# A gated-linear-attention trunk on one core: turning two blocks of rows into columns with 32x32 squares on VectorE

## The chip, the cores and the metric

The kernel runs on one core of a Trainium2 chip. The metric is device time in microseconds (us): the median of three runs. PE is TensorE, DVE is VectorE, ACT is ScalarE, POOL is GpSimd; SP is the engine whose queue issues every DMA of this kernel.

## The reference

One decoder layer on 2048 tokens of 1024 features: gated linear attention, then a gated FFN with a causal convolution, each modulated before (`1 + scale`, `shift`) and normalised after. What matters here is the seam between the two: the attention's normalised rows go through the FFN's modulation and then into a matmul.

```python
def post_norm_residual(x, cs, w_mod, b_mod, ln_gain, ln_bias, sublayer):
    shift, scale, gate = jnp.split((cs @ w_mod + b_mod)[:, None, :], 3, axis=-1)
    y = sublayer(x * (1 + scale) + shift)
    return layer_norm(DN_ALPHA * x + (1 + gate) * y, ln_gain, ln_bias)

def gla_mixer(h, w_in, w_a2, b_a, norm_g, w_o):          # shortened
    q, k, v, r, a_lr = jnp.split(h @ w_in, [qk, 2 * qk, 2 * qk + dv, 2 * qk + 2 * dv], axis=-1)
    log_a = jax.nn.log_sigmoid((a_lr @ w_a2 + b_a)) / GLA_TAU
    # 4 heads, chunks of 64 tokens: att = causal(q_dec k_inv^T); o = att v + q_dec S; S = S * decay + k_dec^T v
    o = o * lax.rsqrt(jnp.mean(o * o, -1, keepdims=True) + LN_EPS) * norm_g
    return (o * jax.nn.silu(r)) @ w_o

def conv_ffn(h, w_up, conv_w, conv_b, w_down):
    u, g = jnp.split(h @ w_up, 2, axis=-1)
    u = causal_depthwise_conv3(u, conv_w) + conv_b
    return (jax.nn.silu(u) * g) @ w_down

x = post_norm_residual(x, cs, mod_w[i, 0], mod_b[i, 0], ln_g[i, 0], ln_b[i, 0], mixer)
x = post_norm_residual(x, cs, mod_w[i, 1], mod_b[i, 1], ln_g[i, 1], ln_b[i, 1], ffn)
```

## The kernel before

**Arithmetic.** Each f32 operand is split into a high part (an ACT cast) and a remainder (a DVE subtraction, line 110), and a product is three matmuls (lines 113 to 115), 128x128 by 128x512.

**Attention.** The tokens go in four blocks of 512 (`tb` 0 to 3, here blocks 1 to 4). Each block runs through 32 weight units of 1 MB (`unit()`): for each pair of heads four of v, then q and k of each head and the r gate; after those eight of the output projection. A unit is loaded by SP into one of four buffers `hl` (line 136, from `wq_d` in block 4), so a load waits until the buffer's last reader on PE is done. Units 0 to 3 of block 4 are v of the first two heads, 4 and 5 q and k of head 0, 6 and 7 q and k of head 1. The work of head 0 beside them is `head_a` (four transposes at line 713, then the products Q by KI) and `head_b` (the products of v by KTt). `at_unit` hangs other work on units of the stream.

**Rows and columns.** The output projection leaves rows: 128 tokens by 1024 features, four tiles `z` for a block. `ln1` normalises them (BN statistics on DVE, the scaling on ACT, line 863) and stores them to `zn_d`. The FFN needs columns: features on the partitions, tokens along the row, times `1 + scale` plus `shift` (`A2`, `B2`). `ln1_out` makes these: a 128x128 transpose on PE with the identity (line 844) into a PSUM bank, four for a tile `kt` of 128 features, then one eviction that also scales and shifts (DVE line 849, or ACT line 847), and a store of 256 KB to `xm2_d` (line 850). Block 1 is turned from reloaded rows (`zc`, line 838), blocks 2 and 3 from the `z` tiles at two units in the next block (for block 3 that is after units 2 and 3 of block 4), block 4 from `zc` in FFN iterations 3 to 6, one pair of tiles in each.

**Token sums.** The FFN is a fast matrix product with seven products of half the size for eight, over two halves of the tokens. `x_pre` makes four of its operands for a half and a pair: four 512 KB loads `xp` from `xm2_d` (line 275), four DVE subtractions (line 281), each with a store to `xt_d` behind it (lines 283 to 289). For the first half it is hung on block 4 (units 4 and 13), for the second on FFN iterations 9 and 12 (`todo`).

**FFN up.** 44 iterations, 22 for each half of the tokens, of seven products of twelve matmuls. The list `todo` hangs the turning on them. In each iteration `w_load` brings the next up-weights (`wu`, `wg`, lines 333 and 334), whose sums are made on DVE an iteration later.

**Order.** The kernel is written as a program; a scheduler of the framework puts each engine's instructions into an order by its own costs, and then each engine runs its order strictly. SP too: a store that waits for DVE holds up every load behind it. `order(later, earlier)` fixes two instructions against each other without a wait.

Of the kernel before, what the change touches and what calls it, by code (L numbers as in the profile page):

```python
# [8 lines left out]
F32 = mybir.dt.float32  # L9
F32R = mybir.dt.float32r  # L10
U32 = mybir.dt.uint32
AF = mybir.ActivationFunctionType
# [4 lines left out]
P = 128  # L17
# [21 lines left out]
def kernel(  # L39
# [46 lines left out]
    def raw_tile(name="raw"):  # L86
        return rawp.tile([P, 1024], F32, tag="raw", name=name)

    def z_tile(name="z"):
        return zp.tile([P, 1024], F32, tag="z", name=name)  # L90
# [21 lines left out]
    def mm3(po, a, b, first, last, resumed=False):  # L112
        nc.tensor.matmul(po, a[0], b[0], start=first, stop=False, skip_group_check=resumed)  # L113
        nc.tensor.matmul(po, a[0], b[1], start=False, stop=False, skip_group_check=resumed)  # L114
        return nc.tensor.matmul(po, a[1], b[0], start=False, stop=last, skip_group_check=resumed)  # L115
# [81 lines left out]
    ws_d = [dram.tile([P, 2, 512], F32, name=f"ws_d{j}") for j in range(NJ)]  # L197
    xt_d = [[[dram.tile([P, 1024], F32, name=f"xt_d{h}_{i}_{r}") for r in range(2)] for i in range(7)] for h in range(2)]
    wq_d = [dram.tile([P, 2, 1024], F32, name=f"wq_d{n}") for n in range(32)]
    xm2_d = [[dram.tile([P, 2, TB], F32, name=f"xm2_d{t}_{k}") for k in range(4)] for t in range(NTB)]  # L200
    G2_d = dram.tile([P, D], F32, name="G2_d")

# [67 lines left out]

    X_AT = ((0, 0), (1, 0), (1, 1), (0, 1))

    def x_raw(hf, n, pr, r):
        half, b = X_AT[n]
        load(r, xm2_d[2 * hf + b][2 * half + pr].rearrange("p k t -> p (k t)"))

    def x_pre(hf, pr):
        b11, b21, b22, b12 = [z_tile("xp") for _ in range(4)]
        for n, r in ((0, b11), (3, b12), (2, b22), (1, b21)):
            x_raw(hf, n, pr, r)  # L280
        sub = lambda o, a, b: nc.vector.tensor_tensor(o, a, b, op=ALU.subtract)
        sub(b11, b12, b11)
        store(xt_d[hf][4][pr], b11)
        sub(b12, b22, b12)
        store(xt_d[hf][6][pr], b12)
        sub(b22, b22, b11)
        store(xt_d[hf][5][pr], b22)
        sub(b21, b21, b22)
        store(xt_d[hf][3][pr], b21)
# [73 lines left out]
    def at_unit(u, fn, *a):  # L363
        steps.setdefault(u, []).append((fn, a))
# [11 lines left out]
    if True:  # L376
# [288 lines left out]
        def gemm_f(xm):  # L665
            w = unit()
            wv = w.rearrange("p s (k c) -> p s k c", k=KT)
            po = psum("mm", 4)
            for kt in range(KT):
                mm3(po, (wv[:, 0, kt], wv[:, 1, kt]), (xm[kt][:, 0], xm[kt][:, 1]), kt == 0, kt == KT - 1)  # L670
            return po

        def gemm_q(xm, E, tick, pq=None):
# [159 lines left out]
        def ln1_out(tb, zs, prs, by_act=False):  # L833
            for pr in prs:
# [4 lines left out]
                for k in range(2):  # L839
# [9 lines left out]
                        nc.vector.tensor_scalar(xt, pt, A2[:, kt:kt + 1], B2[:, kt:kt + 1], op0=ALU.mult, op1=ALU.add)  # L849
                    store(xm2_d[tb][pr][:, k], xt)  # L850

        def normalise(z, after=None):
            st = smp.tile([P, 2, 6], F32, tag="bst", name="bst")
            for i in range(2):
                bn = nc.vector.bn_stats(st[:, i], z[:, i * 512:i * 512 + 512])
                if after is not None:
                    order(bn, after)
            mv = smp.tile([P, 2], F32, tag="mv", name="mv")
            nc.vector.bn_aggr(mv, st)
            rs = smp.tile([P, 2], F32, tag="rs", name="rs")  # L860
            rsqrt_eps(rs[:, 0:1], mv[:, 1:2])
            nc.gpsimd.tensor_scalar(rs[:, 1:2], mv[:, 0:1], rs[:, 0:1], -1.0, op0=ALU.mult, op1=ALU.mult)
            nc.scalar.activation(z, z, AF.Identity, bias=rs[:, 1:2], scale=rs[:, 0:1])
# [28 lines left out]
        for tb in range(NTB):  # L892
            last = tb + 1 == NTB
            b = 32 * tb
            gated = []
            Hs = [dict(h=h, last=last, gated=gated) for h in range(NH)]
            for i, u in ((0, 6), (1, 8), (2, 18), (3, 20)):
                u += b + (tb == 0 and i < 2)
                for k, f in ((0, head_a), (1, head_b), (3, head_c), (5, head_d)):
                    at_unit(u + k, f, Hs[i])  # L900
            at_unit(b + 12, next_decays, (2, 3))
            if tb == 0:
                for k, u in enumerate((10, 10, 11, 11, 11, 12, 14, 15)):
                    at_unit(u, gate_step, 0, k, gs1)
                at_unit(16, gate_end, 0, G1, gs1)
            if tb == 1:
                load(lnc, lncol)
                for n in range(16):
                    at_unit(b + 5 + n, mod_cols, 1, n // 4, (n % 4,))
                    if n % 4 == 3:  # L910
                        at_unit(b + 6 + n, mod_fin, 1, n // 4)
                at_unit(b + 22, mod2)
            if tb == 2:
                for pr in range(4):
                    at_unit(b + 13 + pr, ln1_out, 0, None, (pr,))
                for k in range(8):
                    at_unit(b + 14 + k, gate_step, 1, k, gs2)
                at_unit(b + 22, gate2)
            if tb == 3:
                at_unit(b + 4, x_pre, 0, 0)  # L920
                at_unit(b + 13, x_pre, 0, 1)
                at_unit(b + 25, first_w)
                at_unit(b + 29, lambda: (w_sums1(first["W"]), w_h0(first["W"])))
                at_unit(b + 30, lambda: (w_sums2(first["W"]), w_h2(first["W"])))
            if not last:
                if tb == 0:
                    for pr in range(4):
                        at_unit(b + 25 + pr, next_xm, tb + 1, (pr,))
                else:
                    at_unit(b + 25, next_xm, tb + 1)  # L930
                at_unit(b + 28 + (tb == 0), next_a)
                at_unit(b + 29 + (tb == 0), next_decays, (0, 1))

            pqk = {}
            if tb == 0:
                xm, nxt["A3"], v0, pqk["pq"], pqk["pk"] = gemm_start()
                next_decays((0, 1))
            else:
                v0 = gemm_v(xm, tick)
            for pr in range(2):  # L940
                v = v0 if pr == 0 else gemm_v(xm, tick)
                E = nxt["E"]
                for h in (2 * pr, 2 * pr + 1):
                    H = Hs[h]
                    H["v"], H["el"] = v, E[h][2]
                    H["Q"] = gemm_q(xm, E[h], tick, pqk.pop("pq", None))
                    H["KI"], H["KK"] = gemm_k(xm, E[h], tick, pqk.pop("pk", None))
                for h in (2 * pr, 2 * pr + 1):
                    Hs[h]["sr"] = []
                    for e in range(2):  # L950
                        Hs[h]["sr"].append(gemm_r(xm, tick))
            zs = load_z(tb)
            if 0 < tb < NTB - 1:
                at_unit(b + 32 + 2, ln1_out, tb, zs, range(0, 2))
                at_unit(b + 32 + 3, ln1_out, tb, zs, range(2, 4))
            out_proj(tb, 0, gated, zs, tick)
            if last:
                abx.close()
                up = ctx.enter_context(tc.tile_pool(name="up", bufs=1, reuse_waits="tile"))
                X0, XN = [None] * 7, [None] * 7  # L960
                for i in PROD[:4]:
                    tiles = [x_tile(up, i) for pr in range(2)]
                    x_fill(up, X0, i, x_stage(up, 0, i), tiles)
            out_proj(tb, 1, gated, zs, tick)
            if last:
                zs_last = zs
            else:
                xm = nxt["xm"]
# [11 lines left out]
    if True:  # L980
# [15 lines left out]
        def prod(st, i, po, first):  # L996
            h, half = WHERE[i]
            t = st["W"][h]
            w = [(t[:, 0, half * 512 + k * P:half * 512 + k * P + P],
                  t[:, 1, half * 512 + k * P:half * 512 + k * P + P]) for k in range(4)]  # L1000
            mm = mmk(po, w, st["X"][i], first)
            if st["refill"] is not None:
                x_fill(up if i in PROD[:4] else ur, st["refill"], i, ahead_x.pop(0))
                if len(nextx) > 0:
                    ahead_x.append(x_stage(up, 1, nextx.pop(0)))
            return mm
# [110 lines left out]
        w_h3(W)  # L1117

        nextx, ahead_x = list(PROD), []
        todo = {3 + pr: [(ln1_out, NTB - 1, None, (pr,), True)] for pr in range(4)}  # L1120
        todo |= {9: [(x_pre, 1, 0)], 12: [(x_pre, 1, 1)]}
        G2 = gp.tile([P, D], F32, tag="G", name="G2")
        load(G2, G2_d)
        prev = None
        for n in range(2 * NJ):
# [41 lines left out]
            if prev is not None:  # L1167
                conv_b(prev["h1"], prev["U"], 1, prev["j"])
            pc = st["pc"] = psum("w", 4)
            prod(st, 4, pc, True)  # L1170
            prod(st, 6, pa, False)
            u3, u3i = keep(pa, "u3")
            if prev is not None:
# [245 lines left out]
```

## Time and profile before

| What | Value |
|---|---|
| Median of 3 runs | 2142.45 us (2142.05 to 2142.62) |
| The profiled execution's own time | 2141.68 us |
| Its span | 2139.8 us |
| Granted TensorE clock | 0.998 of full speed |
| Busy: PE, DVE, ACT, POOL | 99%, 67%, 42%, 5% |
| DMA queue of SP | 69.9% of 16 engines |
| Chain that ended last | PE 92%, DVE 3%, DMA 3% |

The trace's times count from the span's start. A matmul of 128x512 shows 0.39 us but follows the last one after 0.227 us, as they overlap; what a group of PE instructions costs is therefore read from the starts of those around it. The span, 2139.8 us, is 1.9 us under the execution's time.

### The profile page before, as it was taken

The page shows a single profiled execution, that of the slowest core. Times are in us where ns is not written, and L with a number is a line of the kernel's source. Part 1 is how long each engine was busy: PE and PEld are TensorE (multiplying, and loading weights), DVE is VectorE, ACT ScalarE, POOL GpSimd, SP SyncE. Part 2 cuts the span into 40 slices and gives each one's busy share as a digit, 9 for nine tenths or more (in the row PEclk, how much of TensorE's full clock was granted, in tenths as well). Part 3 has the DMA queues.
Part 4 walks back from the last instruction along what each step waited for, and adds up shares of the span by engine and source line. Part 5 has one row for each costly group of instructions (what it writes and reads, how often), then busy time and mean ns, then how long its engine had stood idle before and what let it go on. Part 6 is the DMA issues. An engine that isn't in the chain of part 4 may idle for free.

```text
span 2139.8 us, 26750 instructions
## 1 busy us (share of the span) xinstructions
PE 2124.7 (99%) x9916; PEld 1771.1 (83%) x9916; DVE 1423.3 (67%) x2015; ACT 892.6 (42%) x1356; POOL 115.5 (5%) x258
## 2 busy tenths in 40 slices
PE   9999999999999999999999999999999999999998
PEld 7888888888888888888888888888888888888886
DVE  7876576434743553878777778666666797578557
ACT  4655553433343343544444454333333434344332
POOL 0010100010001000000000000000000000021003
PEclk9999999999999999999999999999999999999999
DMA  8477886664866766777855469878777888577562
GB/s 313 165 259 271 315 325 238 222 249 176 296 228 240 263 243 230 256 260 279 308 191 186 172 214 340 295 247 284 249 263 278 268 309 287 193 243 254 191 204 89
DMA packets 155106, 529.28 MB, mean 247 GB/s; under 512 B 17664, under 2 KB 21888, under 8 KB 134752
## 3 DMA queue, kind: packets, MB, share of 16 engines
q1 hardware_dynamic: 154976, 527.58, 69.9%
q8 instruction: 78, 1.28, 0.2%
q14 instruction: 52, 0.43, 0.1%
HBM read 364.72 MB, written 162.79 MB: 247 GB/s over the span
## 4 chain that ended last, share of the span: by engine, by line
PE 92%; DVE 3%; DMA 3%; ACT 1%; issue 1%; SPq 0%; POOL 0%; POOLq 0%; DVEq 0%; ACTq 0%
PE ps_mm L113 22%; PE ps_mm L115 22%; PE ps_mm L114 22%; PE ps_w L114 8%; PE ps_w L115 8%; PE ps_w L113 8%; DMA raw<-in_wab_dram 2%; DMA xraw<-in_xT_dram 1%; PE ps_w L844 1%; DVE hl L110 1%; PE ps_w L602 1%; PE ps_w L793 1%; ACT hl L107 0%; PE ps_w L529 0%; PE ps_w L528 0%
## 5 line engine op out<-in xcount | busy, mean ns | idle before, releaser
L113 PE MATMUL ps_mm<-xc,hl 128*128 128x512 f32 x704 | 274.3, 390 | 0.0
L114 PE MATMUL ps_mm<-xc,hl 128*128 128x512 f32 x704 | 273.9, 389 | 0.0
L115 PE MATMUL ps_mm<-xc,hl 128*128 128x512 f32 x704 | 273.9, 389 | 0.0
L113 PE MATMUL ps_mm<-xm,hl 128*128 128x512 f32 x496 | 194.9, 393 | 0.5 <-DVE v L110 0.5
L115 PE MATMUL ps_mm<-xm,hl 128*128 128x512 f32 x496 | 193.6, 390 | 0.0
L114 PE MATMUL ps_mm<-xm,hl 128*128 128x512 f32 x496 | 193.5, 390 | 0.0
L113 PEld LDWEIGHTS ps_mm<-xc,hl 128*128 128x128 f32 x704 | 132.1, 188 | 27.5 <-ACT u L1010 0.2
L115 PEld LDWEIGHTS ps_mm<-xc,hl 128*128 128x128 f32 x704 | 132.1, 188 | 27.5
L114 PEld LDWEIGHTS ps_mm<-xc,hl 128*128 128x128 f32 x704 | 132.2, 188 | 27.3
L1024 DVE SCALAR_TENSOR_TENSOR ct<-U,cw_sb,ct 128x512 f32<-128x512 f32 x176 | 131.6, 747 | 22.1 <-ACT ct L1018 20.6
L113 PE MATMUL ps_w<-xc,hl 128*128 128x512 f32 x352 | 136.9, 389 | 0.0
L114 PE MATMUL ps_w<-xc,hl 128*128 128x512 f32 x352 | 136.9, 389 | 0.0
L115 PE MATMUL ps_w<-xc,hl 128*128 128x512 f32 x352 | 136.9, 389 | 0.0
L107 ACT CAST dhl<-raw 128x1024 fp32r<-128x1024 f32 x57 | 60.0, 1053 | 152.3 <-PE ps_mm L115 96.0
L1010 ACT COPY u<-ps_mm 128x512 f32<-128x512 f32 x88 | 51.4, 584 | 154.9 <-PE ps_mm L115 152.9
L107 ACT CAST hl<-raw 128x1024 fp32r<-128x1024 f32 (+1 forms) x73 | 70.0, 965 | 108.8 <-PE ps_mm L115 42.2
L110 DVE TENSOR_TENSOR hl<-raw,hl 128x1024 fp32r<-128x1024 f32 (+1 forms) x73 | 81.0, 1116 | 47.3 <-ACT hl L107 47.1
L110 DVE TENSOR_TENSOR dhl<-raw,dhl 128x1024 fp32r<-128x1024 f32 x57 | 69.5, 1219 | 63.8 <-ACT dhl L107 63.8
L115 PEld LDWEIGHTS ps_mm<-xm,hl 128*128 128x128 f32 x496 | 93.2, 188 | 19.9 <-issue 0.2
L113 PEld LDWEIGHTS ps_mm<-xm,hl 128*128 128x128 f32 x496 | 93.2, 188 | 19.7 <-DVE v L110 1.0
L114 PEld LDWEIGHTS ps_mm<-xm,hl 128*128 128x128 f32 x496 | 93.2, 188 | 18.2 <-issue 0.2
L113 PE MATMUL ps_mm<-dhl 128*128 128x512 f32 x264 | 102.7, 389 | 0.0
(246 smaller groups left out, 4998.0 us busy)
## 6 DMA issues: line engine op xcount, KB each, us to landing
hl<-wq_d SPq DMA_DIRECT2D x82, 1024.0 KB, 5.0
hc_d<-ct SPq DMA_DIRECT2D x154, 256.0 KB, 2.6
raw<-hc_d SPq DMA_DIRECT2D x70, 512.0 KB, 4.2
draw<-wc_d SPq DMA_DIRECT2D x70, 512.0 KB, 4.8
wq_d<-hl SPq DMA_DIRECT2D x32, 1024.0 KB, 5.1
raw<-in_wab_dram SPq DMA_DIRECT2D x46, 512.0 KB, 6.4
wu<-in_wup_dram SPq DMA_DIRECT2D x44, 512.0 KB, 5.6
wg<-in_wup_dram SPq DMA_DIRECT2D x44, 512.0 KB, 4.0
```

Source lines behind the costliest of these rows:

```text
L107: accs["copy"] = nc.scalar.copy(h, src)
L110: return nc.vector.tensor_tensor(l, src if lsrc is None else lsrc, h.bitcast(F32), op=ALU.subtract)
L113: nc.tensor.matmul(po, a[0], b[0], start=first, stop=False, skip_group_check=resumed)
L114: nc.tensor.matmul(po, a[0], b[1], start=False, stop=False, skip_group_check=resumed)
L115: return nc.tensor.matmul(po, a[1], b[0], start=False, stop=last, skip_group_check=resumed)
L602: nc.tensor.matmul(po, wv[:, a, kt], xm[kt][:, b], start=kt + a + b == 0, stop=kt == KT - 1 and b == 1)
L793: nc.tensor.transpose(pt[:, s * P:s * P + P], on[:, s, e * P:e * P + P], ident)
L844: nc.tensor.transpose(pt[:, t * P:t * P + P], src, ident)
L1010: return t, nc.scalar.copy(t, po)
L1024: nc.vector.scalar_tensor_tensor(ct, U[:, o + i:o + i + 512], cw_sb[:, j, i:i + 1], ct, op0=ALU.mult, op1=ALU.add)
```

## The change

Blocks 3 and 4 are no longer transposed on PE. DVE transposes each 32x32 square of a row tile and leaves it where it stands (`nc.vector.transpose`, an instruction STREAM_TRANSPOSE of 128x1024): of block 3 into a raw tile `zt` after units 1 and 2 of block 4, of block 4 onto its own `z` tile in FFN iterations 2 to 5. The result goes to a new DRAM tensor `zt_d` in four stores of 512 KB for a block. A column tile `kt` is read back by four DMAs (`cols_in`), each for 32 features by 512 tokens, which put every square in its place: 512 pieces of 128 bytes in each. ACT then scales and shifts in place (`cols_mod`, 128x512), and a store goes to `xm2_d` as before (`cols_out`). Both blocks are read back in the FFN: block 3 in iterations 3 to 10, block 4 in 7 to 14. The token sums of the second half go in two steps, loads in iterations 15 and 17, subtractions and stores in 16 and 18. In block 4 of the attention, `x_pre` for the first half is called as before.

```diff
+    zt_d = [dram.tile([TB, D], F32, name=f"zt_d{t}") for t in range(NTB)]
...
-    def x_raw(hf, n, pr, r):
+    def x_raw(hf, n, pr, r, after=None):
         half, b = X_AT[n]
-        load(r, xm2_d[2 * hf + b][2 * half + pr].rearrange("p k t -> p (k t)"))
-
-    def x_pre(hf, pr):
-        b11, b21, b22, b12 = [z_tile("xp") for _ in range(4)]
+        i = load(r, xm2_d[2 * hf + b][2 * half + pr].rearrange("p k t -> p (k t)"))
+        if after is not None:
+            order(i, after())
+
+    xps = {}
+
+    def x_pre_in(hf, pr, after=None):
+        xps[pr] = b11, b21, b22, b12 = [z_tile("xp") for _ in range(4)]
         for n, r in ((0, b11), (3, b12), (2, b22), (1, b21)):
-            x_raw(hf, n, pr, r)
-        sub = lambda o, a, b: nc.vector.tensor_tensor(o, a, b, op=ALU.subtract)
+            x_raw(hf, n, pr, r, after)
+
+    def x_pre(hf, pr, after=None):
+        if pr not in xps:
+            x_pre_in(hf, pr)
+        b11, b21, b22, b12 = xps.pop(pr)
+        def sub(o, a, b):
+            i = nc.vector.tensor_tensor(o, a, b, op=ALU.subtract)
+            if after is not None:
+                order(i, after())
...
+        def turn_sq(tb, t, z=None):
...
+            zt = raw_tile("zt")
+            order(nc.vector.transpose(zt, z), accs["hl"])
+            turned[tb, t] = zt
+
+        def turn_out(tb, t, after):
+            order(store(zt_d[tb][t * P:t * P + P], turned.pop((tb, t))), after())
+
+        def cols_in(tb, kt, tile, after):
+            if kt % 2 == 0:
+                turned[tb, "x", kt // 2] = tile("xt")
+            xt = turned[tb, "x", kt // 2][:, kt % 2 * 512:kt % 2 * 512 + 512]
+            for g in range(4):
+                c = kt * P + g * 32
+                order(load(xt[g * 32:g * 32 + 32].rearrange("i (b j) -> i b j", j=32),
+                           zt_d[tb][:, c:c + 32].rearrange("(b i) j -> i b j", i=32)), after())
+
+        def cols_mod(tb, kt, after):
+            xt = turned[tb, "x", kt // 2][:, kt % 2 * 512:kt % 2 * 512 + 512]
+            order(nc.scalar.activation(xt, xt, AF.Identity, bias=B2[:, kt:kt + 1], scale=A2[:, kt:kt + 1]), after())
+
+        def cols_out(tb, kt, after):
+            xt = turned[tb, "x", kt // 2][:, kt % 2 * 512:kt % 2 * 512 + 512]
+            order(store(xm2_d[tb][kt // 2][:, kt % 2], xt), after())
...
             if 0 < tb < NTB - 1:
-                at_unit(b + 32 + 2, ln1_out, tb, zs, range(0, 2))
-                at_unit(b + 32 + 3, ln1_out, tb, zs, range(2, 4))
+                if tb == 2 or False:
+                    for t in range(4):
+                        at_unit(b + 32 + 1 + t // 2, turn_sq, tb, t, zs[t])
+                        at_unit(b + 32 + 2 + t // 2, turn_out, tb, t, last_load)
+                else:
+                    at_unit(b + 32 + 2, ln1_out, tb, zs, range(0, 2))
+                    at_unit(b + 32 + 3, ln1_out, tb, zs, range(2, 4))
...
-        todo = {3 + pr: [(ln1_out, NTB - 1, None, (pr,), True)] for pr in range(4)}
-        todo |= {9: [(x_pre, 1, 0)], 12: [(x_pre, 1, 1)]}
+        def turn_here(t):
+            i = nc.vector.transpose(zs_last[t], zs_last[t])
+            order(i, last_h2())
+            turned[NTB - 1, t] = zs_last[t]
+
+        for t in range(4):
+            then(2 + t, turn_here, t)
+            then(3 + t, turn_out, NTB - 1, t, last_h2)
+        for kt in range(KT):
+            for q, n in ((2, 3 + kt), (3, 7 + kt)):
+                then(n, cols_in, q, kt, z_tile, last_h2)
+                then(n + 1, cols_mod, q, kt, last_h2)
+                then(n + 1, cols_out, q, kt, last_h2)
+        for pr in range(2):
+            then(15 + 2 * pr, x_pre_in, 1, pr, last_h2)
+            then(16 + 2 * pr, x_pre, 1, pr, last_h2)
```

Here `last_load` is the newest unit load issued, `last_h2` the last matmul of product 4 of the iteration, and `then(n, f, ...)` hangs `f` on FFN iteration n.

**Three places of the order, all in block 4.** First SP's queue, in the kernel before, from weight unit 7 on. `hl<-wq_d7` and `wq_d8` are the loads of units 7 and 8, `xm2_d2` are the columns of block 3, `xp` and `xt_d` belong to `x_pre`.

```order
L136 DMA hl_6207<-wq_d7_224 128x2048
L850 DMA xm2_d2_2_259<-xt_6130 128x512
L850 DMA xm2_d2_2_259<-xt_6138 128x512
L850 DMA xm2_d2_3_260<-xt_6146 128x512
L850 DMA xm2_d2_3_260<-xt_6154 128x512
L275 DMA xp_6191<-xm2_d0_0_249 128x1024
L275 DMA xp_6194<-xm2_d1_0_253 128x1024
L275 DMA xp_6193<-xm2_d1_2_255 128x1024
L275 DMA xp_6192<-xm2_d0_2_251 128x1024
L283 DMA xt_d0_4_0_197<-xp_6191 128x1024
L136 DMA hl_6240<-wq_d8_225 128x2048
L285 DMA xt_d0_6_0_201<-xp_6194 128x1024
```

The same stretch of SP's queue in the changed kernel, from unit 6 to unit 9; the stores of `zt_d2` lie ahead of it.

```order
L136 DMA hl_6109<-wq_d6_223 128x2048
L276 DMA xp_6143<-xm2_d0_0_253 128x1024
L276 DMA xp_6146<-xm2_d1_0_257 128x1024
L276 DMA xp_6145<-xm2_d1_2_259 128x1024
L276 DMA xp_6144<-xm2_d0_2_255 128x1024
L298 DMA xt_d0_4_0_197<-xp_6143 128x1024
L300 DMA xt_d0_6_0_201<-xp_6146 128x1024
L302 DMA xt_d0_5_0_199<-xp_6145 128x1024
L304 DMA xt_d0_3_0_195<-xp_6144 128x1024
L136 DMA hl_6159<-wq_d7_224 128x2048
L136 DMA hl_6192<-wq_d8_225 128x2048
L136 DMA hl_6258<-wq_d9_226 128x2048
```

The load of unit 7 stood ahead of all of `x_pre`; now it stands behind its four loads and its four stores. Unit 8 stood behind one of the stores; now behind all four.

Second DVE in the changed kernel at the same place: Q of head 0, the four subtractions whose results these stores take (`xp`), and the K products of head 0 (KI).

```order
L696 TENSOR_TENSOR Q32_6136<-Q32_6136,el_5854 128x4x64
L110 TENSOR_TENSOR Q_6140<-Q32_6136,Q_6140 128x768
L293 TENSOR_TENSOR xp_6143<-xp_6146,xp_6143 128x1024
L293 TENSOR_TENSOR xp_6146<-xp_6145,xp_6146 128x1024
L707 TENSOR_TENSOR KI32_6186<-ps_mm_6161,E2_5851 128x512
L293 TENSOR_TENSOR xp_6145<-xp_6145,xp_6143 128x1024
L293 TENSOR_TENSOR xp_6144<-xp_6144,xp_6145 128x1024
L110 TENSOR_TENSOR KI_6188<-KI32_6186,KI_6188 128x512
L712 TENSOR_TENSOR KI32_6186<-KI32_6186,el_5854 128x512
```

Before, one subtraction stood ahead of KI32 and three behind it; now it is two and two. All four still stand behind the split of Q.

Third PE, in the kernel before, where unit 6 gives way to unit 7 (`hl_6207`); `KI32` and `Q` by `KI` are `head_a` of head 0.

```order
L115 MATMUL ps_mm_6242<-xm_5699,hl_6157 128x512
L113 MATMUL ps_mm_6308<-xm_5665,hl_6207 128x512
L114 MATMUL ps_mm_6308<-xm_5665,hl_6207 128x512
L713 MATMUL ps_w_6274<-ident_91,KI32_6234 128x128 x4
L113 MATMUL ps_w_6282<-Q_6188,KI_6236 128x192
```

And in the changed kernel, from the end of `head_a` on; `v` by `KTt` is `head_b`, and unit 7 is `hl_6159`.

```order
L115 MATMUL ps_w_6246<-Q_6140,KI_6188 128x192
L113 MATMUL ps_w_6291<-v_6095,KTt_6231 128x256
L114 MATMUL ps_w_6291<-v_6095,KTt_6231 128x256
L115 MATMUL ps_w_6291<-v_6095,KTt_6231 128x256
L113 MATMUL ps_w_6291<-v_6098,KTt_6231 128x256
L114 MATMUL ps_w_6291<-v_6098,KTt_6231 128x256
L113 MATMUL ps_mm_6260<-xm_5669,hl_6159 128x512
L114 MATMUL ps_mm_6260<-xm_5669,hl_6159 128x512
```

Before, two matmuls of unit 7 came ahead of `head_a` and the other 22 straight after it, with all nine of `head_b` behind them. Now all of `head_a` and five matmuls of `head_b` come ahead of unit 7, and the other four of `head_b` behind its 24.

## Rows read from the trace of the kernel before

**Rows 1.** The page: busy us (share) xinstructions, by engine.

```profile
PE 2124.7 (99%) x9916; PEld 1771.1 (83%) x9916; DVE 1423.3 (67%) x2015; ACT 892.6 (42%) x1356; POOL 115.5 (5%) x258
```

**Rows 2.** PE's timeline: start us, us, engine line op out<-in xcount.

```profile
682.40 0.39 PE L115 MATMUL ps_mm<-hl,xm 128*128 128x512 f32 x1
682.63 1.91 PE L844 MATMUL ps_w<-ident,z 128*128 128x128 f32 x16
684.30 0.48 PE L113 MATMUL ps_mm<-hl,xm 128*128 128x512 f32 x1
...
689.84 1.91 PE L844 MATMUL ps_w<-ident,z 128*128 128x128 f32 x16
```

**Rows 3.** FFN iterations 2, 3, 7: engines' busy us, PEclk, DMA share, GB/s.

```profile
909.54:928.57 19.03, 19.03 (x85) 15.76 (x84) 16.95 (x26) 10.16 (x13) 2.91 (x8) 1.00 0.88 306
928.57:948.51 19.94, 19.94 (x94) 16.59 (x92) 13.11 (x18) 9.36 (x13) 0.28 (x2) 1.00 0.75 274
...
1008.31:1027.35 19.04, 19.04 (x86) 15.77 (x84) 16.25 (x23) 8.03 (x11) 0.28 (x2) 1.00 0.98 350
```

**Rows 4.** DVE's timeline, 669 to 716 us; [idle before <-releaser].

```profile
683.27 2.97 DVE L849 TENSOR_SCALAR xt<-ps_w,A,B 128x512 f32<-128x512 f32 x4 [13.86 <-PE ps_w L844]
...
699.42 0.96 DVE L110 TENSOR_TENSOR Q<-Q,Q 128x768 fp32r<-128x768 f32 x1 [0.90 <-ACT Q L107]
701.35 1.23 DVE L281 TENSOR_TENSOR xp<-xp 128x1024 f32<-128x1024 f32 x1 [0.96 <-DMA xp<-xm_d]
...
703.29 3.74 DVE L281 TENSOR_TENSOR xp<-xp 128x1024 f32<-128x1024 f32 x3
```

**Rows 5.** Timeline of SP's queue: start and us of issuing.

```profile
690.03 0.32 SPq L136 DMA_DIRECT2D hl<-wq_d  x1
...
702.60 0.32 SPq L283 DMA_DIRECT2D xt_d<-xp  x1
703.01 0.38 SPq L136 DMA_DIRECT2D hl<-wq_d  x1
...
707.05 0.32 SPq L289 DMA_DIRECT2D xt_d<-xp  x1
707.47 2.82 SPq L136 DMA_DIRECT2D hl<-wq_d  x2
```

**Rows 6.** PE's timeline around weight unit 7 of block 4.

```profile
708.15 0.39 PE L114 MATMUL ps_mm<-xm,hl 128*128 128x512 f32 x1
...
716.47 0.40 PE L113 MATMUL ps_mm<-xm,hl 128*128 128x512 f32 x1
```

**Rows 7.** Landing of weight unit 0, issued at 645.97 us.

```profile
DMA to landing us min/median/max: 4.7/4.7/4.7
```

**Rows 8.** Landing of weight unit 8, issued at 703.01 us.

```profile
DMA to landing us min/median/max: 6.7/6.7/6.7
```

**Rows 9.** Landing of weight unit 9, issued at 707.47 us.

```profile
DMA to landing us min/median/max: 9.0/9.0/9.0
```

**Rows 10.** DVE by shape, 640 to 720 us: busy us, mean ns.

```profile
L281 DVE TENSOR_TENSOR xp<-xp 128x1024 f32<-128x1024 f32 x4 | 4.9, 1224 | 1.0 <-DMA xp<-xm_d 1.0
...
L513 DVE TENSOR_TENSOR_SCAN az<-smask,mn 128x512 f32<-128x512 f32 x2 | 2.4, 1219 | 0.0
```

**Rows 11.** DMA queue 1.70 to 2.45 us: packets, MB, share of 16 engines.

```profile
q1 hardware_dynamic: 248, 0.02, 20.1%
```

**Rows 12.** DMA queue 917 to 921 us, larger packets.

```profile
q1 hardware_dynamic: 675, 1.31, 100.8%
```

**Rows 13.** DMA of FFN iteration 7: issues, KB each, us to landing.

```profile
xp<-xm_d SPq DMA_DIRECT2D x3, 512.0 KB, 7.9
xt_d<-xp SPq DMA_DIRECT2D x2, 512.0 KB, 6.8
```

**Rows 14.** SP's queue: an up-weight load of iteration 8.

```profile
1030.53 0.33 SPq L334 DMA_DIRECT2D wg<-in_wup_dram  x1
```

**Rows 15.** Tile wg, 1008 to 1047 us: count, ns, first and last start.

```profile
L324 DVE TENSOR_TENSOR s<-wu,wg x3: 681/681/683, 1010.9 to 1044.2; 128x512 f32<-128x512 f32 x3
```

More of the change, by code (lines that the diff above doesn't have):

```diff
@@ L669, in gemm_f @@
             for kt in range(KT):
-                mm3(po, (wv[:, 0, kt], wv[:, 1, kt]), (xm[kt][:, 0], xm[kt][:, 1]), kt == 0, kt == KT - 1)
+                accs["mm"] = mm3(po, (wv[:, 0, kt], wv[:, 1, kt]), (xm[kt][:, 0], xm[kt][:, 1]), kt == 0, kt == KT - 1)
             return po
@@ L850, in ln1_out, with last_load, last_mm @@
                     store(xm2_d[tb][pr][:, k], xt)
+        turned = {}
+        def turn_sq(tb, t, z=None):
+            if z is None:
+                z = raw_tile("zr")
+                load(z, zn_d[tb * 4 + t])
+            zt = raw_tile("zt")
[17 more added lines that the diff above has]
+            order(store(xm2_d[tb][kt // 2][:, kt % 2], xt), after())
+        def last_load():
+            return stream_loads[-1]
+        def last_mm():
+            return accs["mm"]
         def normalise(z, after=None):
@@ L1119, with then, last_h2 @@
         nextx, ahead_x = list(PROD), []
-        todo = {3 + pr: [(ln1_out, NTB - 1, None, (pr,), True)] for pr in range(4)}
-        todo |= {9: [(x_pre, 1, 0)], 12: [(x_pre, 1, 1)]}
+        todo = {}
+        def then(n, f, *a):
+            todo.setdefault(n, []).append((f, *a))
+        def last_h2():
+            return accs["h2"]
+        def turn_here(t):
[13 more added lines that the diff above has]
+            then(16 + 2 * pr, x_pre, 1, pr, last_h2)
         G2 = gp.tile([P, D], F32, tag="G", name="G2")
@@ L1169 @@
             pc = st["pc"] = psum("w", 4)
-            prod(st, 4, pc, True)
+            accs["h2"] = prod(st, 4, pc, True)
             prod(st, 6, pa, False)
```

## The prediction

> **What bounds the kernel now.** I read the page's busy times first: PE works 2124.7 of 2139.8 us, 99% [rows 1], so only two things move the end, work taken off PE and waits put on it. Next came PE's timeline around the transposes and a table by FFN iteration, for the price of what is removed; there the reader is to see that transposes stand between matmuls and push every later one back. Then came the queue of SP, whose order the change alters, and the times from issue to landing of weight loads; there the reader is to see how far ahead of its use each load is issued. A measurement of this kernel can tell about 0.2%, 4.3 us, from no change.
>
> **PE's part.** In block 4's attention, PE turns block 3 in two groups of sixteen [rows 2]. The last matmul ahead of the first group starts at 682.40, the next behind it at 684.30. Without the group these starts would be one pitch of 0.23 us apart, so it costs 1.67 us; the matmul behind it also shows 0.48 us instead of 0.39, another 0.09. The second group at 689.84 looks the same: 2 x 1.76 = 3.5 us. In the FFN, iterations 3 to 6 run from 928.57 to 1008.31, 19.94 us each; iterations 2 and 7, which have no turns, take 19.03 and 19.04 [rows 3]. That is 0.895 us each and 3.6 in all. Nothing else on PE changes in number, so 7.1 us leave an engine that does not wait: **-7.1**. What comes next after each group, a weight unit's matmuls or those of product 4, has its operands by then, since the loads of the units 4 and 5 and the up-weights keep their places ahead of it.
>
> **The load of weight unit 7.** This is the one place where I see a new wait. Before, SP issued it at 690.03 [rows 5], as soon as its buffer came free, and PE took it about 18 us later, as 708.15 is its second matmul [rows 6]. Now it stands behind `x_pre`'s four loads and four stores, and the stores wait for DVE's subtractions, which stand behind the split of Q. I work in the times of before, since PE's gain of 3.5 us shifts DVE's Q and PE alike. The split of Q ends at 699.42 + 0.96 = 700.38 [rows 4]. The first subtraction then waited 0.96 us for its load. In the new order the loads go out ahead of where unit 7's load was, so before 690.03; with the 7.9 us that such loads took in a busy stretch [rows 13] they land by 698, and that wait goes. The four subtractions and KI32 between them ended at 703.29 + 3.74 = 707.03; they now end 0.96 earlier, at 706.07. The last store goes out at once, as at 707.05 before, and the next load 0.42 us after it [rows 5]: unit 7 is issued at 706.5 instead of 690.03.
>
> How long it then takes is bounded by three loads of the same size. Unit 0, with little else under way, took 4.7 us [rows 7]; unit 8, right behind one such store (702.60, then 703.01), took 6.7 [rows 5, 8]; unit 9, behind another store and with unit 8's load still coming in, took 9.0 [rows 9]. Ahead of the new unit 7 there are stores, but no other weight load, so I take 6.7: it lands at 713.2. PE has by then done `head_a` and the five matmuls of `head_b` that the new order puts ahead, and waits. From 713.2 on it has 24 matmuls of 0.227 us, 5.4, and four narrower ones at about half, 0.5, until unit 8 begins: 719.1, where before it began at 716.47 [rows 6]. **+2.6**, with 0.6 for the quiet landing and 4.9 for 9.0. Unit 8 itself is issued about 0.4 us behind unit 7; even at 9.0 us it lands at 715.9, ahead of 719.1. PE is the bound behind it, so what is lost here does not come back.
>
> **The squares on DVE.** The trace has no such instruction. A subtraction of the same 128x1024 took 1.224 us, and a scan took 1.219 for 512 columns, so 2.44 for 1024 [rows 10]; as a floor, half the subtraction, 0.6. I take 1.22, since the shape and type are the subtraction's. For block 3, four make 4.9 us, at most 9.8, and DVE stood idle 13.86 us just there, waiting for PE's transposes [rows 4]; the eight evictions that followed go too (four of them 2.97 us). For block 4, one falls in each of iterations 2 to 5, where DVE is busy 16.95 us of 19.03 in the fullest, iteration 2 [rows 3]: 2.1 us are free. At 1.22 that is hidden, at 2.44 it is 0.4 over. I take 0, with +0.4 at one end. If PE waited for every one of them in full, it would be 4 x 1.22 = 4.9; that is a rival below.
>
> The Trainium skill, on the page "VectorE: DVE Perf Modes", section "The three transpose paths", gives 311 ns on VectorE for 128x128 in bf16 and only 32x32 squares. Eight such would be 2.49 us, an estimate from that page; the sum would then be -4.1 instead of -4.5. No row of before shows the instruction, so the trace can't decide it.
>
> **The column loads.** 64 DMAs read `zt_d` in pieces of 128 bytes, 512 pieces each. Iterations 7 to 10 have eight of them, 4096 pieces or 256 for each of the 16 engines; iterations 3 to 6 and 11 to 14 have half. What a piece costs lies between two rows. From 1.70 to 2.45 us only packets under 512 bytes ran: 248 of them took 20.1% of 16 engines over 0.75 us, 9.7 ns each [rows 11]. From 917 to 921 us 675 packets of 1.9 KB on average took 100.8% over 4 us, 96 ns each [rows 12]. I take 9.7 by size: 2.5 us in the fullest iterations, 24.5 at the other end. The fullest stretch of before is iteration 7 with a DMA share of 0.98 [rows 3]; but five of its transfers, three loads and two stores of 512 KB [rows 13], are `x_pre` of the second half, which moves to iterations 15 to 18. They are 2.6 of the 6.7 MB (350 GB/s by 19.04 us), so about 0.60 is left, 11.4 us, and 13.9 with the new pieces. There is room: **0**. Issuing takes SP 0.32 us at rest and 1.41 with a full queue [rows 5]; eight make 2.6 to 11.3 us of an iteration. Nor does PE wait for what they bring before the second half's sums, which now come in iterations 15 to 18, ahead of the second half. The sixteen scalings on ACT lie beside 8.0 to 10.2 us of ACT work in 19 us [rows 3], and they replace eight evictions there.
>
> **The sum.** -7.1 + 2.6 = -4.5 on the profiled execution's 2141.68: 2137.2. The median of the runs stands 0.8 above that execution, so 2137.9.
>
> **The rivals.**
> Unit 7 is not late. If the load lands like a quiet one, or DVE's subtractions come sooner than I place them, only 0 to 0.6 is lost: -7.1, 2135.3. For it: the stores ahead are spread over more than 4 us. Against: the order puts the load behind the last subtraction, and Q's split bounds that.
>
> Unit 7 lands like unit 9. Units 8 and 9 are issued on its heels and share the engines: 9.0 us, 4.9 lost, -2.2: 2140.2, within 0.2%. For it: three loads and two stores in a row. Against: unit 9 had another weight load ahead of it, unit 7 has none.
>
> DVE is the pace in iterations 2 to 5. PE takes the split weights from DVE in every iteration; if the squares stand in that chain and not in its free time, 4.9 come back: +0.4, 2142.8. For it: only 2.1 us are free in iteration 2. Against: 5.9 us are free in iteration 3.
>
> Small pieces hold up the queue, on the slower side. The up-weights come on the same queue; one issued at 1030.53 is first read at 1044.2 [rows 14, 15], 13.7 us later, so with a landing of 7.9 there are 5.8 to spare. A piece at 52.6 ns, midway between the ends, makes 13.5 us for each engine; with 11.4 of other traffic that is 24.9 in 19.04, 5.9 too many. Over iterations 7 to 10 that is 23.4, less 5.8: 17.6 lost, 2155.5. It decides from the point where the excess passes the slack, at about 36 ns a piece. For it: 675 packets filled 4 us [rows 12], and here 4096 come on top in 19. Against: small packets cost 9.7 ns where they are seen.
>
> The Trainium skill speaks against such loads: "DMA: Bandwidth & Descriptors", section "Rules for kernel authors", wants no transpose by a plain DMA with a rearranged pattern and puts the difference at 19 times. Eight loads of 64 KB at the 350 GB/s of iteration 7 are 1.5 us; 19 times that is 28.5, an estimate, and would cost more than this rival. The rows show no such load; here each piece stays whole, as the squares were turned on DVE, and that is why I give it little.
>
> **How the numbers follow.** My forecast 0.48, not late 0.18, like unit 9 0.14, DVE the pace 0.07, small pieces 0.13. The line for faster is 2138.2, just above my 2137.9; a landing of up to 7.0 us stays under it, and I give that 0.58 of my case. Faster: 0.28 + 0.18 = 0.46. Same: 0.20 + 0.14 + 0.07 = 0.41. Slower: 0.13. My case alone runs from 2136.5 to 2139.5; the range of 2135.0 to 2143.0 takes in the three rivals that stay near and leaves out the small pieces.
>
> **What would show it.** Right: no transposes of `z` or `zc` on PE after 640 us; iterations 3 to 6 at 19.04 us; a PE wait of 1 to 3 us for the load of unit 7, just behind the first matmuls of `head_b`, and that load issued behind the fourth `xt_d` store. Squares near 1.2 us. Wrong: no such gap, or other gaps, above all in iterations 3 to 14 with DMA shares near 1, and column loads that take long to land.

## The result, and the profile after

The changed kernel takes 2155.87 us (median of 4 runs, 2154.75 to 2156.94) against 2142.25 for the kernel before on the same chip: a ratio of 1.0062, interval 1.005 to 1.0075, 13.6 us slower. The forecast was 2137.9, with a range of 2135.0 to 2143.0.

The head of the page after, to be held against [rows 1]: span; busy us of the engines; the chain that ended last.

```profile
span 2153.1 us, 26672 instructions
...
PE 2123.9 (99%) x9852; PEld 1766.4 (82%) x9852; DVE 1427.8 (66%) x2015; ACT 899.0 (42%) x1364; POOL 113.5 (5%) x258
...
PE 85%; DMA 6%; DVE 5%; ACT 2%; issue 1%; SPq 0%; POOL 0%; POOLq 0%; DVEq 0%; ACTq 0%
```

PE has its 64 instructions fewer, but its busy time fell by only 0.8 us, and the chain lost PE's share to DMA, DVE and ACT. What PE waited for behind 640 us, total, times, longest:

```profile
PE ps_mm L113 <- ACT hl L107: 11.0, 3, 5.8
PE ps_mm L113 <- DMA hl<-wq_d: 1.8, 1, 1.8
PE ps_mm L113 <- ACT u L1067: 0.7, 1, 0.7
```

Before, this table is empty. The second line is the wait that was forecast; the first is new, and the FFN's stretches show where it is (columns as in [rows 3]; the last two are pieces of the second row):

```profile
945.47:964.51 19.04, 19.04 (x86) 15.77 (x85) 15.05 (x20) 8.73 (x12) 0.28 (x2) 1.00 0.57 202
1040.67:1068.39 27.72, 21.87 (x85) 17.14 (x84) 17.44 (x24) 10.53 (x16) 0.28 (x2) 0.88 0.67 209
1068.39:1089.34 20.95, 19.62 (x86) 15.61 (x84) 13.47 (x18) 9.13 (x13) 0.28 (x2) 1.00 0.59 162
1089.34:1115.66 26.32, 22.32 (x85) 17.44 (x84) 15.39 (x21) 9.53 (x13) 0.28 (x2) 0.87 0.68 221
1057.70:1061.00 3.30, 3.22 (x7) 2.12 (x8) 3.21 (x4) 1.00 (x2) 0.00 (x0) 0.50 0.77 176
1065.00:1069.00 4.00, 4.00 (x19) 3.34 (x18) 2.63 (x5) 1.69 (x4) 0.00 (x0) 1.00 0.95 392
```

The iterations that used to turn block 4 now take 19.04 us (the first line is one of four). Three later ones take 27.72, 20.95 and 26.32: 8.68 + 1.91 + 7.28 = 17.9 us too many. The reader should see two things beside it. The DMA share there is 0.59 to 0.68, not near 1. And two of the three have a granted clock below 0.9: 0.50 right behind the wait, 1.00 some microseconds on.

Counting the split matmuls, 9288 in both kernels, and setting the start of the same number side by side gives the whole account:

| Matmul | Before | After | Ahead (-) or behind |
|---|---|---|---|
| attention, ahead of block 3's turn | 663.59 | 663.09 | -0.50 |
| first of weight unit 8 | 716.47 | 714.55 | -1.92 |
| FFN, start of iteration 3's window | 928.35 | 926.43 | -1.92 |
| behind iteration 6 | 1008.08 | 1002.59 | -5.49 |
| ahead of the first long window | 1046.16 | 1040.67 | -5.49 |
| behind the three | 1103.28 | 1115.66 | +12.38 |
| behind the FFN's up part | 1712.66 | 1725.92 | +13.26 |

Up to iteration 9 the changed kernel has gained 5.0 beside the 0.5 that it had from its start, half a microsecond more than the forecast sum of 4.5. Then it loses 17.9, and 0.9 in a wait for an ACT copy where the up part ends.

### The profile page after: what moved, and what is told of

It is laid out like the page before. It is cut to its first block, busy times and chain, and to the rows that moved or that the text cites. A ratio compares the mean times of both kernels' runs of the same rounds, so it can differ in the third digit from the quotient of the medians.

```text
span 2153.1 us, 26672 instructions
## 1 busy us (share of the span) xinstructions
PE 2123.9 (99%) x9852; PEld 1766.4 (82%) x9852; DVE 1427.8 (66%) x2015; ACT 899.0 (42%) x1364; POOL 113.5 (5%) x258
## 4 chain that ended last, share of the span: by engine, by line
PE 85%; DMA 6%; DVE 5%; ACT 2%; issue 1%; SPq 0%; POOL 0%; POOLq 0%; DVEq 0%; ACTq 0%
PE ps_mm L113 20%; PE ps_mm L115 20%; PE ps_mm L114 20%; PE ps_w L114 7%; PE ps_w L115 7%; PE ps_w L113 7%; DMA raw<-in_wab_dram 3%; DVE hl L110 1%; DMA xraw<-in_xT_dram 1%; ACT hl L107 1%; DMA xp<-xm_d 1%; PE ps_w L808 1%; DMA zt_d<-zt 0%; DMA wu<-in_wup_dram 0%; PE ps_w L859 0%
## 5 line engine op out<-in xcount | busy, mean ns | idle before, releaser
L1075 ACT ACTIVATE ct<-U,cb_sb,cw_sb 128x512 f32<-128x512 f32 x88 | 71.6, 813 | 76.3 <-DVE U L339 76.3
```

What stands on the lines that cost most here:

```text
L1075: nc.scalar.activation(ct, U[:, o + 2:o + 514], AF.Identity, bias=cb_sb[:, j:j + 1], scale=cw_sb[:, j, 2:3])
```

## Where PE waits

The first of the three waits. PE's timeline:

```profile
1051.55 0.39 PE L115 MATMUL ps_w<-xc,hl 128*128 128x512 f32 x1
1057.74 0.80 PE L113 MATMUL ps_mm<-xc,hl 128*128 128x512 f32 x1 [5.81 <-ACT hl L107]
1058.34 0.63 PE L114 MATMUL ps_mm<-xc,hl 128*128 128x512 f32 x1
...
1062.92 0.39 PE L114 MATMUL ps_mm<-xc,h 128*128 128x512 f32 x1
```

ACT's, just ahead of it:

```profile
1056.64 1.04 ACT L107 CAST hl<-wu 128x1024 fp32r<-128x1024 f32 x1 [2.35 <-DMA wu<-in_wup_dram]
```

SP's queue, one iteration:

```profile
1038.54 0.34 SPq L371 DMA_DIRECT2D wh_d<-hl  x1
...
1043.59 0.46 SPq L887 DMA_DIRECT2D xt<-zt_d  x1
...
1048.96 0.44 SPq L896 DMA_DIRECT2D xm_d<-xt  x1
1049.46 2.12 SPq L887 DMA_DIRECT2D xt<-zt_d  x4
1051.63 0.49 SPq L348 DMA_DIRECT2D wu<-in_wup_dram  x1
```

PE stands before the first product of iteration 10, whose weights ACT casts from `wu` at 1056.64; ACT waited for that load, and SP issued it at 1051.63. Before, the same load was issued at 1019.38 and first read at 1044.2. The order shows why. Before, around that load (`wu_8993`), and after (`wu_8917`):

```
L356 DMA wh_d8_153<-hl_8808 128x2048          (before)
L333 DMA wu_8993<-in_wup_dram 128x1024

L896 DMA xm2_d3_0_265<-xt_8749 128x512        (after)
L887 DMA xt_8749<-zt_d3_252 32x16x32 x3
L371 DMA wh_d9_154<-hl_8855 128x2048
...
L896 DMA xm2_d2_2_263<-xt_8756 128x512
L887 DMA xt_8756<-zt_d2_251 32x16x32 x4
L348 DMA wu_8917<-in_wup_dram 128x1024
```

SP works ahead of the other engines; its longest stops are at the store `wh_d`, one in each iteration, which waits for DVE's split of that iteration (22.9 us in four stops between 1020 and 1120 us). Before, the load for iteration n stands right behind `wh_d` of n - 2, from iteration 3 to the end of the first half. After, up to iteration 9, it still stands behind `wh_d` of n - 2, but with up to 12 other transfers between; for 10 to 13 it stands behind `wh_d` of n - 1. Call the time from a load's issue to its first read its lead. It went in two steps: in iterations 7 to 9 from between 26 and 29 us down to between 15 and 18, which cost nothing, and in 10 to 13 from 24.9 down to between 4.7 and 9.4. For iteration 10, the load above, it is 5.0. The slipped loads belong to the iterations around those with eight column loads; for 14 the old stop and a lead of 15 are back.

The loads themselves were not slow. This is the time from issue to landing of `wu` for iterations 10 to 12, after and then before:

```profile
DMA to landing us min/median/max: 4.5/4.9/5.2
DMA to landing us min/median/max: 5.9/6.0/8.2
```

With the column loads ahead of them they landed sooner than before. They were issued too late.

## The experiments

**1. The column loads on ACT's queue.** Edit:

```
-    order(load(xt[g * 32:g * 32 + 32]..., zt_d[tb][...]...), after())
+    order(nc.scalar.dma_start(xt[g * 32:g * 32 + 32]..., zt_d[tb][...]...), after())
```

> The changed kernel, with the 64 column loads issued from ACT's queue instead of SP's; pieces and bytes stay the same. In SP's order the up-weights of FFN iterations 10 to 13, which the change puts one place of wh_d later than before, are back in their old place. Theory A (SP's order: the loads of up-weights stand behind column loads and stores that wait): the three PE waits at the start of iterations 10 to 12 and the slow clock behind them go, 17.9 us: about 2138 us, 4 to 5 us faster than before; the wait for weight unit 7 (2.1 us) stays. Rival B (the 128-byte pieces fill the DMA engines): the same pieces still run in the same iterations, the waits stay, 2150 us or more. Rival C (ACT is held up by issuing): new PE waits for ACT casts, anything above 2142.

Measured 2142.59 us, ratio 1.0001 (0.9992 to 1.001). PE's waits from 900 to 1200 us:

```profile
PE ps_w L115 <- DVE hl L110: 1.6, 3, 0.5
PE ps_mm L113 <- ACT p L1067: 0.7, 1, 0.7
```

The 11.0 us of waits for `wu`'s cast are gone, though the same pieces run in the same iterations: rival B falls. Four small new waits between 1030 and 1095 us cost 0.85 us of span each; with the wait for unit 7 still there (2.1 us), that is why it only draws level. One of the four is rival C's: ACT spent 3.69 us on issuing four column loads, from 1064.62 on, and the copy that PE waited for came behind them. The other three are DVE's: in its new order the split of `wg` stands behind four sums, the first of which waits for PE, while ACT's cast was long done.

**2. The first `x_pre` of block 4 three units later.** Edit: `at_unit(b + 4, x_pre, 0, 0)` becomes `at_unit(b + 7, ...)`.

> The changed kernel, with the first x_pre of block 4 hung on weight unit 7 instead of 4, so that the loads of weight units 7 to 11 stand ahead of it on SP; the FFN's order is not touched. Theory A: the wait of PE for unit 7 goes, 2.6 us, and the three FFN waits stay: 2155.9 - 2.6 = 2153.3 us. Rival B (the load of unit 7 is not what PE waited for, or the next load behind x_pre is late instead): 2155 to 2158 us.

Measured 2152.52 us, ratio 1.0048 (1.0036 to 1.006). PE's waits, 640 to 800 us:

```profile
PE ps_w L113 <- ACT KTt L107: 1.2, 1, 1.2
PE ps_w L115 <- DVE KTt L110: 0.2, 1, 0.2
```

The cast of `KTt` on ACT:

```profile
728.01 0.58 ACT L107 CAST KTt<-ps_w 128x512 fp32r<-128x512 f32 x1 [4.04 <-DMA xt_d<-xp]
```

The wait for unit 7 is gone, and PE is 4.8 us ahead of before by matmul 3072; but then it waits for `KTt` of head 1, and 1.9 come back. `KTt` is given the buffer that held the first `xp` tile, and ACT may write it only when the store of that tile has landed; with `x_pre` moved, that store is late. The three FFN waits are as they were (11.0 us). So the wait for unit 7 was the load's, as theory A has it, but in the profile most of it came back from a place that neither theory named. The median is 3.3 below the changed kernel's; the two intervals overlap.

**3 and 4. One block alone.** Edits: only block 3, `then(3 + pr, ln1_out, NTB - 1, None, (pr,), True)` in place of block 4's lines; only block 4, `if tb == 2 or False` becomes `if False`, and block 3's column loads go.

> Only block 3 is turned by squares; block 4 is transposed on PE as before, in FFN iterations 3 to 6. Four column loads in each of iterations 3 to 10. Up-weights keep their old place on SP. Theory A: -3.5 (transposes) - 0.4 (the wait of head_a's transposes) + 2.6 (unit 7) and no FFN wait: 2142.25 - 1.4 = 2140.9 us. Rival B (pieces): iterations 3 to 10 each carry half of what 7 to 10 carry in the changed kernel, so some of the 17.9 us stays: 2144 us or more.

> Only block 4 is turned by squares (in place, FFN iterations 2 to 5), read back in iterations 7 to 14, four column loads in each; block 3 is transposed on PE as before, and the load of unit 7 stands ahead of x_pre as before. Theory A: -3.6 us and nothing else: 2138.7 us. Rival B (pieces): waits in iterations 7 to 14, 2142 us or more. Rival D (the squares on DVE hold up PE in iterations 2 to 5): those iterations longer than 19.04 us, up to 4.9 us in all, 2143 us.

Measured 2141.34 us, ratio 0.9993 (0.9984 to 1.0001), for block 3 alone and 2139.46, ratio 0.9984 (0.9976 to 0.9993), for block 4: 1.4 and 3.3 us under the 2142.76 of the kernel before beside them. Block 3's only wait behind 640 us, and a matmul of unit 7 just behind it:

```profile
PE ps_mm L113 <- DMA hl<-wq_d: 1.9, 1, 1.9
...
709.94 0.63 PE L113 MATMUL ps_mm<-xm,hl 128*128 128x512 f32 x1
```

Block 4 has no wait in the FFN and gains 3.6 there by the count of matmuls, as the sum said. Block 3 alone can't be told from no change: its interval takes in 1, and in the profile nothing is left of its 3.5, since unit 7 cost 3.8 there instead of the 2.1 of the changed kernel (behind the wait some matmuls ran at half the clock, 0.63 us instead of 0.39). What the two runs do show is the FFN without a wait. The up-weight loads of iterations 10 to 13 moved back in SP's order here too, to leads of 11 to 15 us, but none crossed a `wh_d`. Only both blocks together, with eight column loads in an iteration, push them past it.

**5. The late place alone.** The kernel before, with the loads for iterations 10 to 13 pinned:

```
+        i = load(wu, wup[2 * j])
+        if hf == 0 and 10 <= j <= 13:
+            order(i, accs["ws"])          # the last store of ws_d
+            order(i, accs["late"])        # the last store of hid_late
```

> The kernel before, all blocks transposed on PE, with nothing changed but SP's order: the up-weight loads of FFN iterations 10 to 13 stand behind the stores wh_d, ws_d and the late hc_d store of one iteration later, about where the changed kernel has them, with no column loads in the queue. Theory A1 (the late place alone makes the waits): the loads are issued around 1050, 1063, 1085 us, land 5 to 6 us later, and PE waits in iterations 10 to 12, 3 us or more in all: 2145 us or more. Theory A2 (the late place takes the lead away, and the waits come from what stands on SP beside it, column loads and stores that wait for ACT): landing 1055 against a first use of 1056 to 1060 just holds, 2142.5 to 2144 us.

Measured 2144.67 us, ratio 1.0014 (1.0005 to 1.0022). In the profile PE loses 4.8 us there, in two waits for ACT's copy of `u` and in matmuls at half the clock behind the second:

```profile
PE ps_mm L113 <- ACT u L1013: 2.5, 2, 1.9
...
1096.14 1.05 ACT L107 CAST hl<-wu 128x1024 fp32r<-128x1024 f32 x1 [3.47 <-DMA wu<-in_wup_dram]
...
1099.97 0.63 PE L115 MATMUL ps_mm<-xc,h 128*128 128x512 f32 x1
```

ACT's copy, at 1097.81, stands behind the cast of `wu`, and the cast waited for the load. No column load is in this queue, so the late place by itself makes waits; but it makes a quarter of the 17.9. The time lies between A1's 2145 and A2's 2144; the waits are A1's in kind and a little under its 3 us in size.

**6. Both queues mended.** Block 3's column loads on ACT's queue, block 4's on SP's, and `x_pre` on unit 6:

```
+    ld = nc.scalar.dma_start if tb == 2 else load
-    at_unit(b + 4, x_pre, 0, 0)
+    at_unit(b + 6, x_pre, 0, 0)
```

> The changed kernel with block 3's column loads on ACT's queue and block 4's on SP's (no iteration has more than four on either), and the first x_pre of block 4 hung on weight unit 6. In SP's order the up-weights have their old place and units 7 to 10 stand ahead of x_pre. Theory A: 7.1 us of transposes and 0.4 of head_a's wait saved, no new wait: before - 7.5, about 2135 us. Rival C (column loads on ACT's queue hold up ACT): PE waits for ACT in iterations 3 to 10, 2138 us or more. Rival B (pieces): 2145 us or more.

Measured 2138.87 us, ratio 0.9982 (0.9973 to 0.9991). The FFN is as theory A has it, 3.6 us ahead and no wait in iterations 3 to 14. In the attention a wait took the other's place:

```profile
PE ps_w L728 <- DVE KI L712: 2.6, 1, 2.6
```

The subtractions, moved to unit 6, now hold up the K product of head 1: DVE waits for their loads until 714.63, and the K product stands behind them in its order. Rivals B and C had no part in the FFN's iterations 3 to 14; as in run 2, moving the work of `x_pre` made a wait that no theory named.

**7. Block 4 one iteration later.** Edit: `(3, 7 + kt)` becomes `(3, 8 + s)`, with the columns of each half's pairs in turn, and `x_pre` in 16 to 18.

> The changed kernel with block 4 read back in iterations 8 to 15 instead of 7 to 14, so that eight column loads fall in three iterations (8 to 10) instead of four; x_pre of the second half moves by an iteration. In SP's order the up-weights slip behind wh_d from iteration 11 on instead of 10. Theory A: the first PE wait comes one iteration later and one of three goes: 2 to 11 us less than the changed kernel, 2145 to 2154 us, waits at the start of iterations 11 and 12 only. Rival B (pieces): the same bytes, spread over one iteration fewer of overlap, about a quarter less of 17.9 us, 2151.5 us, spread over iterations 8 to 10.

Measured 2145.17 us, ratio 1.0011 (1.0002 to 1.002). PE's waits, 900 to 1200 us:

```profile
PE ps_mm L113 <- ACT hl L107: 3.3, 2, 2.0
PE ps_mm L115 <- DVE hl L110: 1.0, 2, 0.5
```

Two waits instead of three, before iterations 11 and 12, as the place of the loads in SP's order says; in the profile 5.5 us are lost there instead of 17.9. The first of the three has gone, and the others are shorter. The profiled execution took 2142.85 us, 2.3 less than the median; where the median's 2.3 go is not shown.

**8 and 9. The stores alone moved.** As run 6, but `x_pre` keeps its loads and subtractions at unit 4, where DVE has room, and only its four stores are hung on unit 5, or 6:

```
+    at_unit(b + 4, x_pre, 0, 0, None, True)     # loads and subtractions
+    at_unit(b + 5, x_out, 0, 0)                 # the four stores
```

> As the kernel with both queues mended, but the first x_pre of block 4 stays at weight unit 4 with its loads and subtractions, and only its four stores are hung on unit 5: the load of unit 7 stands ahead of the stores, unit 8 behind them. DVE keeps the four subtractions where the changed kernel has them. Theory A (PE waited for unit 7 only because its load stood behind stores that wait for DVE): the wait goes, no new one: before - 7.5, about 2134.5 us. Rival B (the wait moves to unit 8, which still stands behind the stores): up to 2.6 us back, 2137 us. Rival C (the wait is DVE's, whose subtractions hold up the K products): a wait for KI or KTt instead, 2137 to 2138 us.

> The same with the four stores hung on unit 6: the loads of units 7 and 8 both stand ahead of them, and the scheduler puts the splits of head 0's K behind the split of head 1's Q on DVE, and head_a's transposes one weight unit later on PE. Theory A: no wait for a weight load; -7.5 again, 2134.5 us. Rival C: head_a of head 1 waits for KI on DVE, 1 to 3 us back, 2136 to 2138 us.

Measured 2134.55 us, ratio 0.9964 (0.9951 to 0.9976), and 2134.62, ratio 0.9966 (0.9952 to 0.998). Run 8's SP queue, to be held against [rows 5]:

```profile
682.89 3.46 SPq L276 DMA_DIRECT2D xp<-xm_d  x4
688.10 0.32 SPq L136 DMA_DIRECT2D hl<-wq_d  x1
697.72 4.58 SPq L311 DMA_DIRECT2D xt_d<-xp  x4
```

Unit 7 is issued at 688.10, ahead of the stores, and behind 640 us PE waits for nothing. This is the forecast sum without the two late loads, -7.5: both versions are 7.5 us faster than the kernel before, and both intervals lie clear of 1. Neither rival B nor C came, in either.

## Why the prediction was wrong

- **PE's part, -7.1: right.** Block 4's four iterations went from 19.93 to 19.04 (3.6), and by the count of matmuls PE is 3.5 further ahead behind block 3's two groups (-4.0, with the 0.5 from its start). Runs 8 and 9 hold both parts with nothing lost: 7.5 by the median, 7.0 to 7.3 by the count up to iteration 9, less what each was ahead from its start. A gap of 0.2 ahead of `head_a`'s transposes (starts at 708.15 and 708.57 before, a pitch being 0.23) goes as well; the forecast left it out, and the 0.4 in the expectations above is twice too much.
- **Weight unit 7, +2.6: right in its chain, a little too large.** SP and PE after:

```profile
682.69 3.27 SPq L276 DMA_DIRECT2D xp<-xm_d  x4
...
701.76 0.32 SPq L304 DMA_DIRECT2D xt_d<-xp  x1
702.18 12.42 SPq L136 DMA_DIRECT2D hl<-wq_d  x5
```

```profile
706.37 0.28 PE L114 MATMUL ps_w<-v,KTt 128*128 128x256 f32 x1
708.47 0.50 PE L113 MATMUL ps_mm<-xm,hl 128*128 128x512 f32 x1 [1.81 <-DMA hl<-wq_d]
...
714.55 0.40 PE L113 MATMUL ps_mm<-xm,hl 128*128 128x512 f32 x1
```

  Issued 0.42 us behind the fourth store, landed within 6.3 (6.7 forecast). At the end of unit 6 PE was 4.0 us ahead of before; at unit 8, 716.47 - 714.55 = 1.9: lost 2.1. The chain of it, four stores that wait for DVE, is what run 8 took away.
- **The squares on DVE, 0: right.** 1.22 us taken; the trace after has them at 1.23 and 1.24, and PE waits for none:

```profile
L875 DVE STREAM_TRANSPOSE zt<-z x4: 1189/1234/1247, 668.1 to 673.8; 128x1024 f32<-128x1024 f32 x4
```

```profile
L1186 DVE STREAM_TRANSPOSE z<-z x4: 1235/1236/1240, 921.2 to 976.0; 128x1024 f32<-128x1024 f32 x4
```

  The estimate by proportion from the Trainium skill's bf16 square ("VectorE: DVE Perf Modes", section "The three transpose paths") was 2.49; the measurement decides, half of that for f32.
- **The column loads, "There is room: 0": wrong, and this is the step that failed.** As transfers they did have room. Half of the 64 landed within 2.8 us, the slowest in 7.3:

```profile
L887 SPq DMA_DIRECT2D xt<-zt_d x64: 377/545/2066, 943.5 to 1175.7; - x64
...
DMA to landing us min/median/max: 2.3/2.8/7.3
```

  A piece cost at most about twice my 9.7 ns. From 1033 to 1037 us, where 1600 of 1728 packets were under 512 bytes, the queue shows

```profile
q1 hardware_dynamic: 1728, 0.46, 49.7%
```

  which is 31.8 us of engine time, at most 20 ns a piece; the rival of the small pieces needed 36. The DMA share of iterations 7 and 8 was 0.63 and 0.57, under the 0.73 of my sum (13.9 of 19.04 us).

  I priced the engines' time and SP's issuing time and set them against an iteration. What I did not look at is where SP's new order puts everything else. I had read this very thing in block 4, a load behind stores that wait, and did not count it through the FFN; of the up-weights the prediction says only that they keep their places. There the loads for iterations 10 to 13 slip behind one more `wh_d`, and that cost 17.9 us where the sum had 0. The order alone showed it.
- **The rivals.** "Small pieces hold up the queue" gave 2155.5, within half a microsecond of the result, and is wrong all the same: its cause was the engines' time for pieces, and run 1 keeps the pieces and loses the 11.0 us of waits, while the late `wu` loads landed in 5 us with the pieces ahead of them. The agreement is chance. The Trainium skill's rule against a plain DMA with a rearranged pattern ("DMA: Bandwidth & Descriptors", section "Rules for kernel authors") had leaned the same way; here pieces of 128 bytes were not the trouble, the DMA share in the three long windows being 0.59 to 0.68.

What is shown: the late place of the loads makes waits (run 5), the pieces in themselves do not (run 1), and the loads cross a `wh_d` only where SP has eight column loads in an iteration (runs 3, 4 and 7). Of the 17.9 us, PE stood still for 6.0, 1.4 and 4.1, which is the gaps between matmuls (6.19, 1.65, 4.35) less a pitch of 0.23, 11.5 in all. The other 6.4 lie right behind these stops (2.7, 0.5 and 3.2), in short second gaps and, behind the first and third, in matmuls at half the clock.

Why the waits are so much longer than in run 5 is shown only in part. There the first late load was issued at 1050.08, here at 1051.63 in a kernel that is 5.5 us ahead, so 7 us later by PE's work. Of these 7, 5.8 are there at the stop itself: `wh_d` of iteration 9 goes out at 1038.54 here and at 1038.26 in run 5, because DVE in its new order makes the sums ahead of that split later. The column loads and the store that waits for ACT, between the stop and the load, add only 1.3. Why DVE's order came out so was not tested. And in the new PE order four matmuls of iteration 10's first product stand ahead of twelve that had their operands.

## What to carry to other kernels

When an edit adds transfers to a queue that one engine issues in order, don't stop at their bytes and packets. Count, iteration by iteration, how many of the old loads still stand ahead of the queue's fixed stop; a load that crosses it loses about an iteration of lead at once (25 us became 6 in run 5, at 19 us an iteration). And where a store waits for a slow producer, move the store, not the work: here moving the stores alone gave the full gain, and moving the work (runs 2 and 6) traded one wait for another.

## What the runs showed that I had not expected

PE's granted clock fell to half, 1.2 GHz, behind the idle stretches of 6.0 and 4.1 us: matmuls of 0.63 us and 0.50 in the window 1057.70 to 1061.00, and the pitch was back at 0.23 by 1062.92. Together with the short gaps between the first matmuls this cost 2.7 us on top of the first wait (8.68 - 5.96).

The length of the stop alone does not tell when this happens. Behind 1.4 us (second wait), 1.9 (unit 7) and 2.2 (run 7) the clock stayed at 1.00. Behind 2.1 us in run 5 and 2.0 at the same unit 7 in run 3 it fell to 0.50, for seven matmuls of 0.63 us each. So the same wait cost 2.1 us in one execution and 3.8 in another, and a wait that looks short in one profile is not safely cheap in the next.
